# Where the late attention gates are multiplied in, and how many buffers the output units' rows have

## The chip, the cores and the metric

The kernel runs on one core of a Trainium2 chip. The metric is the time of one execution in device microseconds (us); lower is better. A run is one timed execution, and a profiled execution is one more that the hardware profiler recorded.

## The reference

One layer of a hybrid encoder. The input x (2048 rows of 1024) is RMS-normalised and projected once. The columns of the projection feed two groups of heads, and both groups end in a gate:

```python
proj = h @ w_in
(dn_q, dn_k, dn_v, dn_z, dn_beta, dn_decay, sw_q, sw_k, sw_v, sw_z) = split(proj, cuts)
dn = gated_deltanet_bidir(...)                  # 4 heads of 128, forward and backward scans
dn = rms_norm(dn, dn_out_norm_w) * silu(dn_z)
sw = windowed_gqa_with_sinks(...)               # 8 query heads of 64, |i-j| <= 128
sw = sw * silu(sw_z)
x = x + concat([dn, sw]) @ w_out
```

The change concerns sw * silu(sw_z): a product of two arrays of 2048 rows by 512 channels, in fp32.

## The kernel before

All arithmetic is fp32. For the matrix products each operand is split into a high and a low part, so that one product is three matmuls. The sequence is cut into 16 chunks of 128 rows (chunk c), and into four blocks b of 512 rows. Channels of the attention output are four groups f of 128 (two heads each).

**Phase A** (lines 75 to 455) runs over the two halves of the sequence. It makes q, k, v by projections, and for each chunk the windowed attention (`attend`). Beside these, as filler for TensorE, it makes the convolved inputs of the delta rule (`conv_pair`) and the gates of the first half (`gate_pairs`). For chunks 0 to 7 `attend` loads the finished gate (zc, line 407), multiplies on GpSimd (POOL, line 408) and stores the gated output. For chunks 8 to 15 the gates do not exist yet, and the raw output is stored (line 409).

**The late gates** (`late_gates`, lines 230 to 247) make the gates of blocks 2 and 3: sixteen tiles (i, b) in the order of LATE, of which the first eight (i below 4) are attention gates and the others belong to the delta rule (zdn). Each tile takes 24 matmuls into one of three PSUM banks (tag "pj"), a tanh on ACT (line 245), a multiply-add on VectorE (DVE, line 246) and a store (line 247). The tile in SBUF, o, comes from the pool zp, a ring of four buffers with the tag "big". The late gates are traced between the first `pre_front` and the first `solve` of phase B.

**Phase B** goes over the four delta-rule heads h. `pre_front(h)` transposes k, v and q, sums squares on ACT into ssk and ssq (line 690, its throw-away output is jk), and builds the chunks' matrices ma. `solve` inverts 32-row triangles on DVE (lines 749 and 753), `invert` joins them by matmuls (line 781), and `scan(h)` runs forward and backward over the chunks with the state S (lines 821 to 859). `post` normalises the scan's output with squares again (line 873, throw-away output jko) and multiplies by zdn (line 890).

**The output's units** (`sw_units`, lines 564 to 608) are the filler of phase B: 32 units (c, j), each the product of chunk c of the gated attention output with one half j of w_out. A unit loads mx (line 583), for chunks 8 to 15 also the gate zcs (line 586) and multiplies on POOL (line 587), splits into mh and ml (lines 590 and 591), loads a piece of x as xr (named xrs in the trace, line 593), runs 12 matmuls (pcs, lines 596 to 598), adds (line 599) and stores the partial result (line 600). The buffers: mx, mh and ml one each (SWB), and a ring of two (SWW) with the tag "ws" that xr, zcs and the pieces of w_out share. Eight units are traced in each of `pre_front(1)` to `pre_front(3)`, and eight after the last of them.

Last, `out_pair` multiplies the delta rule's output with its part of w_out and adds the partial results.

**What sets the order.** `set_order` plans all instructions of the five queues (TensorE, DVE, ACT, POOL, and SP, which issues all DMAs) at once: it knows the dependences, the rings of buffers and estimates of the durations, goes forward and backward several times, and writes the best order out. Each queue then runs in exactly that order. In the plan an SP transfer is done 2.4 us plus its bytes' time after its issue, a tile of a ring waits for all users of the tile that had its buffer, and no tile begins before the one ahead of it in the ring has begun.

Of the kernel before, what the change touches and what calls it, by code (L numbers as in the profile page):

```python
# [15 lines left out]
P = 128  # L16
# [13 lines left out]
SCRATCH = 1024  # L30
NEG = -1e30
FILLF = ((0, 0, 0, 8), (0, 0, 0, 8), (0, 0, 0, 8))
SWB = (1, 1)
SWW = 2


def tile_hybrid(ctx, tc, t, out, dbg=None):
    nc = tc.nc
    V, A, G, T = nc.vector, nc.scalar, nc.gpsimd, nc.tensor
    dma = nc.sync.dma_start  # L40

    cp = ctx.enter_context(tc.tile_pool(reuse_waits="tile", name="cp", bufs=1))
    gp = ctx.enter_context(tc.tile_pool(reuse_waits="tile", name="gp", bufs=1))
    hp = ctx.enter_context(tc.tile_pool(reuse_waits="tile", name="hp", bufs=2))
    dp = ctx.enter_context(tc.tile_pool(reuse_waits="tile", name="dp", bufs=1, space=DRAM))

    def const(name, shape, src=None, dt=F32):
        a = cp.tile(shape, dt, tag=name, name=name)
        if src is not None:
            dma(a, src)  # L50
        return a

    ident = const("ident", [P, P], t["ident"])
    nw = const("nw", [P, KC], t["nwt"])
    bd = const("bd", [P, NCH, 16])
    mix_sw = [dp.tile([P, 4, P], F32, tag=f"mix_sw{c}", name=f"mix_sw{c}") for c in range(NCH)]
    kq_d = [dp.tile([P, 2, S], F32, tag=f"kq_d{h}", name=f"kq_d{h}") for h in range(4)]
    v_d = [dp.tile([P, S], F32, tag=f"v_d{h}", name=f"v_d{h}") for h in range(4)]
    zdn_d = [dp.tile([P, S], F32, tag=f"zdn{i}", name=f"zdn{i}") for i in range(4)]
    zsw_d = dp.tile([4, P, S], F32, tag="zsw_d", name="zsw_d")  # L60

    mix_dn = dp.tile([4, P, S], F32, tag="mix_dn", name="mix_dn")

    with ExitStack() as cb, ExitStack() as wide:
        with tc.using_default_side("right"):
            xe = cb.enter_context(tc.tile_pool(reuse_waits="tile", name="xe", bufs=1))
            ae = cb.enter_context(tc.tile_pool(reuse_waits="tile", name="ae", bufs=1))
        with ExitStack() as ca:
            consts, late = phase_a(ca, wide, xe, ae, tc, t, ident, nw, bd, gp, mix_sw, kq_d, v_d, zdn_d, zsw_d, dp)
        phase_b(cb, wide, xe, ae, late, tc, t, ident, consts, hp, mix_dn, mix_sw, kq_d, v_d, zdn_d, zsw_d, dp, out)  # L70
    if dbg is not None:
        dbg(tc, locals())


def phase_a(ctx, wide, xe, ae, tc, t, ident, nw, bd, gp, mix_sw, kq_d, v_d, zdn_d, zsw_d, q_pool):
    nc = tc.nc
    V, A, G, T = nc.vector, nc.scalar, nc.gpsimd, nc.tensor
    dma = nc.sync.dma_start
# [151 lines left out]
    def late_gates(zp):  # L230
        held = []
        for i, b in LATE:
            w = next((w for j, w in held if j == i), None)
            if w is None:
                w = [wz.tile([P, KC, P], F32R, tag=k, name=f"{k}{i}_{b}") for k in ("zhi", "zlo")]
                col = (16 + i) // 2 if i < 4 else (8 + i) // 2
                for kk in range(0, KC, 2):
                    st = wz.tile([P, 2, P], F32, tag="zst", name=f"zs{i}_{b}_{kk}", bufs=2)
                    dma(st, t["wt"][col][:, kk : kk + 2, i % 2 * P : (i % 2 + 1) * P])
                    A.activation(w[0][:, kk : kk + 2], st, AF.Copy)  # L240
                    V.tensor_tensor(w[1][:, kk : kk + 2], st, w[0][:, kk : kk + 2].bitcast(F32), ALU.subtract)
                held = (held + [(i, w)])[-2:]
            ps = proj_feat(w, 0, b, f"z{i}_{b}")
            o = zp.tile([P, 512], F32, tag="big", name=f"zo{i}_{b}")
            A.activation(o, ps, AF.Tanh, scale=0.5)
            V.scalar_tensor_tensor(o, o, 1.0, ps, ALU.add, ALU.mult)
            dma((zsw_d[i] if i < 4 else zdn_d[i - 4])[:, b * 512 : (b + 1) * 512], o)

    def conv_pair(i0, half):
        w = load_w(t["wt"][i0 // 2], 2 * P, f"c{i0}_{half}")  # L250
# [107 lines left out]
    def attend(c, q2):  # L358
# [4 lines left out]
        for g in range(2):  # L363
            pr = [sp.tile([P, 3 * P], F32, tag="pr", name=f"pr{c}_{g}_{j}", bufs=6) for j in range(4)]
            st = sp.tile([P, 3, 4], F32, tag="st", name=f"st{c}_{g}")
            nm, den, es = (st[:, i] for i in range(3))
            for j in range(4):
                hh = 4 * g + j
                ps = pss.tile([P, 3 * P], F32, tag="pss", name=f"s{c}_{hh}")
                T.matmul(ps[:, :n], q2[g][:, j], k2[:, g, 0, k0 : k0 + n], start=True, stop=False)  # L370
                T.matmul(ps[:, :n], q2[g][:, j], k2[:, g, 1, k0 : k0 + n], start=False, stop=True)  # L371
                V.tensor_tensor_reduce(  # L372
                    pr[j][:, :n], ps[:, :n], mask[:, lo * P : hi * P], 1.0, sink[:, hh : hh + 1],
                    ALU.add, ALU.min, accum_out=nm[:, j : j + 1],
                )
                A.activation(  # L376
                    pr[j][:, :n], pr[j][:, :n], AF.Exp, bias=nm[:, j : j + 1], scale=-1.0, accum_out=den[:, j : j + 1]
                )
            V.tensor_tensor(es, nm, sink[:, 4 * g : 4 * g + 4], ALU.subtract)
            A.activation(es, es, AF.Exp)  # L380
            V.scalar_tensor_tensor(den, den, 1.0, es, ALU.mult, ALU.add)
            V.tensor_scalar(den, den, 2.0, None, ALU.mult)
            V.reciprocal(den, den)  # L383
            for j in range(4):
                G.tensor_scalar(pr[j][:, :n], pr[j][:, :n], den[:, j : j + 1], 1.0, ALU.mult, ALU.mult)  # L385
            po = pso.tile([P, 512], F32, tag="pso", name=f"po{c}_{g}")
            for kb in range(lo, hi):
                pt = pst.tile([P, 4, P], F32, tag="pst", name=f"pt{c}_{g}_{kb}")
                for j in range(4):
                    T.transpose(pt[:, j], pr[j][:, (kb - lo) * P : (kb - lo + 1) * P], ident)  # L390
                ph = sp.tile([P, 512], F32R, tag="ph", name=f"ph{c}_{g}_{kb}")
                pl = sp.tile([P, 512], F32R, tag="pl", name=f"pl{c}_{g}_{kb}")
                ptf = pt.rearrange("p a b -> p (a b)")
                A.activation(ph, ptf, AF.Copy)  # L394
                V.tensor_tensor(pl, ptf, ph.bitcast(F32), ALU.subtract)  # L395
                vk = v2[:, sl - 1 + kb, g]
                T.matmul(po, vk, ph, start=(kb == lo), stop=False)
                T.matmul(po, vk, pl, start=False, stop=(kb == hi - 1))
            ot = sp.tile([P, 2, P], F32, tag="ot", name=f"ot{c}_{g}")
            pv = po.rearrange("p (a b n) -> p a b n", a=2, b=2)  # L400
            A.activation(ot[0:64], pv[64:128, :, 0], AF.Copy)
            A.activation(ot[64:128], pv[64:128, :, 1], AF.Copy)
            V.tensor_tensor(ot[0:64], pv[0:64, :, 0], ot[0:64], ALU.add)
            V.tensor_tensor(ot[64:128], pv[0:64, :, 1], ot[64:128], ALU.add)
            if c < HC:
                zc = sp.tile([P, 2, P], F32, tag="zc", name=f"zc{c}_{g}", bufs=1)
                dma(zc, zsw_d[2 * g : 2 * g + 2, :, c * P : (c + 1) * P].rearrange("f p s -> p f s"))
                G.tensor_tensor(ot, ot, zc, ALU.mult)
            dma(mix_sw[c][:, 2 * g : 2 * g + 2], ot)

    pend = []
    nfill = ((2, 1, 1, 1, 1, 1, 1, 2), (1, 1, 1, 1, 1, 1, 0, 0))
# [134 lines left out]
def phase_b(ctx, wide, xe, ae, late, tc, t, ident, consts, hp, mix_dn, mix_sw, kq_d, v_d, zdn_d, zsw_d, dp, out):  # L547
# [16 lines left out]
    def sw_units(pool):  # L564
# [12 lines left out]
        def unit(c, j, bank):  # L577
# [3 lines left out]
            ns = slice(j * 512, (j + 1) * 512)  # L581
            mx = pool.tile([P, 4, P], F32, tag="mx", name=f"mxs{c}_{j}", bufs=SWB[0])
            dma(mx, mix_sw[c])
            if c >= HC:
                zc = pool.tile([P, 512], F32, tag="ws", name=f"zcs{c}_{j}").rearrange("p (f s) -> p f s", f=4)
                dma(zc, zsw_d[:, :, c * P : (c + 1) * P].rearrange("f p s -> p f s"))
                G.tensor_tensor(mx, mx, zc, ALU.mult)
            mh = pool.tile([P, 4, P], F32R, tag="mh", name=f"mhs{c}_{j}", bufs=SWB[1])
            ml = pool.tile([P, 4, P], F32R, tag="ml", name=f"mls{c}_{j}", bufs=SWB[1])
            A.activation(mh, mx, AF.Copy)  # L590
# [50 lines left out]
    def pre_front(h):  # L641
# [12 lines left out]
        for n, c4 in enumerate(FRONT):  # L654
# [24 lines left out]
            for j, ss in ((0, ssk), (1, ssq)):  # L679
# [6 lines left out]
                for c in range(4):  # L686
                    cc = 4 * c4 + c
                    src = ks[c4] if j == 0 else tr
                    jk = q1.tile([P, P], F32, tag="jk", name=f"jk{h}_{c4}_{j}_{c}", bufs=3)
                    A.activation(jk, src[:, c], AF.Square, accum_out=ss[:, cc : cc + 1])  # L690
            V.tensor_scalar(ssk[:, s4], ssk[:, s4], EPS, None, ALU.add)  # L691
            G.tensor_tensor(nk[:, s4], ssk[:, s4], pw[:, 0, :4], ALU.pow)  # L692
# [171 lines left out]
    def post(h, H, groups):  # L864
# [4 lines left out]
        so = rp.tile([P, 2, 8], F32, tag="so", name=f"sso{nm}")  # L869
        for k, c4 in enumerate(groups):  # L870
            for c in range(4):
                jk = rp.tile([P, P], F32, tag="jko", name=f"jko{nm}_{k}_{c}", bufs=3)
                A.activation(jk, H["oacc"][c4][:, c], AF.Square, accum_out=so[:, 0, 4 * k + c : 4 * k + c + 1])
        s1 = so[:, 1].rearrange("p (g c) -> p g c", c=4)
        V.tensor_scalar(s1, of(H["ssq"]), EPS, 128.0 * EPS, ALU.add, ALU.mult)
# [541 lines left out]
```

## Time and profile before

| | |
|---|---|
| median of 3 runs | 1264.79 us (1262.38 to 1271.20) |
| profiled execution, its own time | 1270.01 us |
| its span, first to last instruction | 1268.0 us |
| mean granted TensorE clock | 0.989 |
| busy: TensorE / weight loads / DVE / ACT / POOL | 95% / 82% / 75% / 57% / 42% |
| late gates' attention tiles: tanh at | 671.2 to 728.5 us |
| units: first to last matmul | 797.1 to 1169.9 us |

In the profile's rows L587 is line 587 of the kernel, and out<-in names what an instruction writes and reads. PE is TensorE's matmul, PEld its weight load, DVE VectorE, ACT ScalarE, POOL GpSimd, and SPq an instruction of SyncE's queue, here mostly the issue of a DMA. A row of waits reads: who waited, for whom, total us, times, longest us.

### The profile page before, as it was taken

How to read it: one execution, taken by the hardware profiler on the slowest of the kernel's cores; microseconds unless marked ns; L12 is line 12 of the kernel's file. 1: busy time of each engine (PE TensorE's matmuls, PEld its weight loads, DVE VectorE, ACT ScalarE, POOL GpSimd, SP SyncE). 2: the span in 40 equal slices, each digit the busy share in tenths (PEclk: the TensorE clock that was granted, in tenths of full speed). 3: DMA queues.
4: the chain of work that ended last, by engine and by line, in shares of the span. 5: the costliest groups of instructions: out<-in, count | busy, mean ns of one | idle time of the engine just before them, and what ended most of it. 6: DMA issues, size and time to landing. Idle time of an engine off the chain costs nothing.

```text
span 1268.0 us, 22351 instructions
## 1 busy us (share of the span) xinstructions
PE 1210.5 (95%) x7018; PEld 1037.4 (82%) x7018; DVE 953.7 (75%) x2320; ACT 725.8 (57%) x2167; POOL 529.2 (42%) x845
## 2 busy tenths in 40 slices
PE   6999999999999999999999998999889899999898
PEld 5998888788889988887777777888789689888776
DVE  4523689999854379999995587698769779876765
ACT  6432476666534367766665438658557845685421
POOL 2243454763302276556422304613742441670541
PEclk9999999999999999999999999999889999999999
DMA  7553243513544434431016848967955875854785
GB/s 259 172 160 125 75 154 100 173 60 102 166 145 125 144 110 137 137 96 55 34 51 207 238 141 245 264 189 207 268 166 174 236 200 152 242 175 122 238 269 199
DMA packets 232294, 206.39 MB, mean 163 GB/s; under 512 B 49137, under 2 KB 181873, under 8 KB 232177
## 3 DMA queue, kind: packets, MB, share of 16 engines
q1 hardware_dynamic: 232176, 204.97, 53.0%
q8 instruction: 56, 0.92, 0.3%
q14 instruction: 62, 0.50, 0.1%
HBM read 139.84 MB, written 65.08 MB: 162 GB/s over the span
## 4 chain that ended last, share of the span: by engine, by line
PE 67%; DVE 13%; DMA 9%; ACT 4%; issue 3%; POOL 1%; SPq 1%; DVEq 0%; ACTq 0%; POOLq 0%
PE pf_c L199 5%; PE pf_c L201 5%; PE pf_c L200 5%; PE pf_z L199 4%; PE pf_z L200 4%; PE pf_z L201 4%; PE pi L781 3%; PE pq_q L212 2%; PE pq_q L211 2%; PE pt L390 2%; PE pq_q L210 2%; DMA xc<-x_d 2%; PE py L830 2%; PE po L839 2%; PE pcs L596 2%
## 5 line engine op out<-in xcount | busy, mean ns | idle before, releaser
L199 PE MATMUL pf_c<-xhi,wh_c 128*128 128x512 f32 x384 | 155.7, 405 | 0.8 <-DVE acc L269 0.8
L200 PE MATMUL pf_c<-xlo,wh_c 128*128 128x512 f32 x384 | 154.7, 403 | 0.0
L201 PE MATMUL pf_c<-xhi,wl_c 128*128 128x512 f32 x384 | 154.3, 402 | 0.0
L269 DVE SCALAR_TENSOR_TENSOR acc<-pf_c,cw,acc 128x512 f32<-128x512 f32 (+1 forms) x192 | 140.8, 742 | 2.6 <-POOL acc L259 0.7
L385 POOL TENSOR_SCALAR pr<-pr,st 128x384 f32<-128x384 f32 (+1 forms) x128 | 79.4, 639 | 98.0 <-DVE st L383 71.2
L394 ACT ACTIVATE ph<-pt 128x512 fp32r<-128x512 f32 x92 | 53.0, 595 | 60.5 <-PE pt L390 51.5
L376 ACT ACTIVATE pr<-pr,st 128x384 f32<-128x384 f32 (+1 forms) x128 | 76.2, 597 | 17.8 <-DVE st L372 17.4
L199 PEld LDWEIGHTS pf_c<-xhi,wh_c 128*128 128x128 f32 x384 | 72.5, 189 | 13.5 <-DVE acc L269 1.3
L201 PEld LDWEIGHTS pf_c<-xhi,wl_c 128*128 128x128 f32 x384 | 72.3, 188 | 12.9
L200 PEld LDWEIGHTS pf_c<-xlo,wh_c 128*128 128x128 f32 x384 | 72.4, 188 | 11.6
L835 ACT ACTIVATE yk<-py,ck 128x128 f32<-128x128 f32 x120 | 43.9, 366 | 62.0 <-PE py L830 61.2
L372 DVE CUSTOM_DVE_ANT_0 pr<-s,mask,sink 128x384 f32<-128x384 f32 (+1 forms) x128 | 73.4, 593 | 2.5 <-PE s L371 1.0
L211 PE MATMUL pq_q<-wh_q,xlo 128*128 128x256 f32 x256 | 72.1, 282 | 0.0
L212 PE MATMUL pq_q<-wl_q,xhi 128*128 128x256 f32 x256 | 71.9, 281 | 0.0
L210 PE MATMUL pq_q<-wh_q,xhi 128*128 128x256 f32 x256 | 71.4, 280 | 0.0
L390 PE MATMUL pt<-ident,pr 128*128 128x128 f32 x368 | 69.5, 274 | 1.8 <-DVE pl L395 1.1
L395 DVE TENSOR_TENSOR pl<-pt,ph 128x512 fp32r<-128x512 f32 x92 | 61.6, 681 | 6.1 <-ACT ph L394 5.6
L390 PEld LDWEIGHTS pt<-ident,pr 128*128 128x128 f32 x368 | 47.8, 140 | 20.4 <-DVE pl L395 4.4
L596 PE MATMUL pcs<-wohs,mhs 128*128 128x512 f32 x128 | 58.3, 456 | 4.4 <-ACT mhs L590 2.7
L692 POOL TENSOR_TENSOR nk<-ssk,pw 128x4 f32<-128x4 f32 x16 | 16.5, 1029 | 106.8 <-DVE ssk L691 106.6
L597 PE MATMUL pcs<-wohs,mls 128*128 128x512 f32 x128 | 56.1, 438 | 1.7 <-DVE mls L591 1.7
L598 PE MATMUL pcs<-wols,mhs 128*128 128x512 f32 x128 | 55.0, 429 | 0.0
(324 smaller groups left out, 4029.4 us busy)
## 6 DMA issues: line engine op xcount, KB each, us to landing
kqc<-kq_d SPq DMA_DIRECT2D x120, 128.0 KB, 3.1
ws_c<-wt SPq DMA_DIRECT2D x48, 256.0 KB, 3.5
xr<-x SPq DMA_DIRECT2D x16, 512.0 KB, 5.3
k_q<-kq_d SPq DMA_DIRECT2D x16, 512.0 KB, 5.6
mxs<-mix_sw SPq DMA_DIRECT2D x32, 256.0 KB, 3.7
xrs<-x SPq DMA_DIRECT2D x32, 256.0 KB, 3.7
part<-xrs SPq DMA_DIRECT2D x32, 256.0 KB, 2.6
xrd<-part SPq DMA_DIRECT2D x32, 256.0 KB, 4.1
```

Of the source, the lines that this page charges most:

```text
L199: T.matmul(ps, hi[:, k, cs], xhi[b][:, k], start=(k == 0), stop=False)
L200: T.matmul(ps, hi[:, k, cs], xlo[b][:, k], start=False, stop=False)
L201: T.matmul(ps, lo[:, k, cs], xhi[b][:, k], start=False, stop=(k == KC - 1))
L210: T.matmul(ps[:, :n], xh, hi[:, k, :n], start=(k == 0), stop=False)
L211: T.matmul(ps[:, :n], xl, hi[:, k, :n], start=False, stop=False)
L212: T.matmul(ps[:, :n], xh, lo[:, k, :n], start=False, stop=(k == KC - 1))
L269: V.scalar_tensor_tensor(av, ps[:, lo:], cw[:, i, k : k + 1], av, ALU.mult, ALU.add)
L372: V.tensor_tensor_reduce(pr[j][:, :n], ps[:, :n], mask[:, lo * P : hi * P], 1.0, sink[:, hh : hh + 1], ALU.add, ALU.min, accum_out=nm[:, j ...
L376: A.activation(pr[j][:, :n], pr[j][:, :n], AF.Exp, bias=nm[:, j : j + 1], scale=-1.0, accum_out=den[:, j : j + 1])
L385: G.tensor_scalar(pr[j][:, :n], pr[j][:, :n], den[:, j : j + 1], 1.0, ALU.mult, ALU.mult)
L390: T.transpose(pt[:, j], pr[j][:, (kb - lo) * P : (kb - lo + 1) * P], ident)
L596: T.matmul(ps, mh[:, k], wh[:, k], start=(k == 0), stop=False)
```

## The change

- The eight late gates of attention (i below 4 in `late_gates`) now load the raw attention output of their channels and block (mxl, from the same ring zp), multiply it in on POOL and store the gated product. The delta rule's gates stay as they were.
- For that the raw output of chunks 8 to 15 is stored to new DRAM tensors raw_d, laid out by channel group, and the gated product to gat_d, laid out by chunk; `mix_sw[c]` of those chunks is a view of gat_d.
- The units of chunks 8 to 15 load the gated rows and no longer load or multiply a gate.
- mx has two buffers (SWB).
- jk and jko have one buffer each where they had three.

```diff
-SWB = (1, 1)
+SWB = (2, 1)
...
-    mix_sw = [dp.tile([P, 4, P], F32, tag=f"mix_sw{c}", name=f"mix_sw{c}") for c in range(NCH)]
+    mix_sw = [dp.tile([P, 4, P], F32, tag=f"mix_sw{c}", name=f"mix_sw{c}") for c in range(HC)]
...
-    zsw_d = dp.tile([4, P, S], F32, tag="zsw_d", name="zsw_d")
+    zsw_d = dp.tile([4, P, HC * P], F32, tag="zsw_d", name="zsw_d")
+    raw_d = [dp.tile([P, 4, 4, P], F32, tag=f"raw_d{b}", name=f"raw_d{b}") for b in (2, 3)]
+    gat_d = [dp.tile([P, 4, 4, P], F32, tag=f"gat_d{b}", name=f"gat_d{b}") for b in (2, 3)]
+    mix_sw += [gat_d[c // 4][:, c % 4] for c in range(HC)]
...
             A.activation(o, ps, AF.Tanh, scale=0.5)
             V.scalar_tensor_tensor(o, o, 1.0, ps, ALU.add, ALU.mult)
-            dma((zsw_d[i] if i < 4 else zdn_d[i - 4])[:, b * 512 : (b + 1) * 512], o)
+            if i < 4:
+                mx = zp.tile([P, 512], F32, tag="big", name=f"mxl{i}_{b}")
+                dma(mx, raw_d[b - 2][:, i].rearrange("p c s -> p (c s)"))
+                G.tensor_tensor(o, o, mx, ALU.mult)
+                dma(gat_d[b - 2][:, :, i], o.rearrange("p (c s) -> p c s", c=4))
+            else:
+                dma(zdn_d[i - 4][:, b * 512 : (b + 1) * 512], o)
...
-            dma(mix_sw[c][:, 2 * g : 2 * g + 2], ot)
+            dma(mix_sw[c][:, 2 * g : 2 * g + 2] if c < HC else raw_d[c // 4 - 2][:, 2 * g : 2 * g + 2, c % 4], ot)
...
             dma(mx, mix_sw[c])
-            if c >= HC:
-                zc = pool.tile([P, 512], F32, tag="ws", name=f"zcs{c}_{j}").rearrange("p (f s) -> p f s", f=4)
-                dma(zc, zsw_d[:, :, c * P : (c + 1) * P].rearrange("f p s -> p f s"))
-                G.tensor_tensor(mx, mx, zc, ALU.mult)
...
-                    jk = q1.tile([P, P], F32, tag="jk", name=f"jk{h}_{c4}_{j}_{c}", bufs=3)
+                    jk = q1.tile([P, P], F32, tag="jk", name=f"jk{h}_{c4}_{j}_{c}", bufs=1)
...
-                jk = rp.tile([P, P], F32, tag="jko", name=f"jko{nm}_{k}_{c}", bufs=3)
+                jk = rp.tile([P, P], F32, tag="jko", name=f"jko{nm}_{k}_{c}", bufs=1)
```

More of the change, by code (lines that the diff above doesn't have):

```diff
@@ L68, in tile_hybrid @@
         with ExitStack() as ca:
-            consts, late = phase_a(ca, wide, xe, ae, tc, t, ident, nw, bd, gp, mix_sw, kq_d, v_d, zdn_d, zsw_d, dp)
+            consts, late = phase_a(ca, wide, xe, ae, tc, t, ident, nw, bd, gp, mix_sw, kq_d, v_d, zdn_d, zsw_d, raw_d, gat_d, dp)
         phase_b(cb, wide, xe, ae, late, tc, t, ident, consts, hp, mix_dn, mix_sw, kq_d, v_d, zdn_d, zsw_d, dp, out)
@@ L72, in tile_hybrid, with phase_a @@
         dbg(tc, locals())
-def phase_a(ctx, wide, xe, ae, tc, t, ident, nw, bd, gp, mix_sw, kq_d, v_d, zdn_d, zsw_d, q_pool):
+def phase_a(ctx, wide, xe, ae, tc, t, ident, nw, bd, gp, mix_sw, kq_d, v_d, zdn_d, zsw_d, raw_d, gat_d, q_pool):
     nc = tc.nc
```

## The prediction

> **What bounds the kernel now.** I first cut the span into four stages with the busy time of each engine (columns: stretch and its length, then busy time and instruction count of PE, PEld, DVE, ACT, POOL, then granted TensorE clock, DMA share, GB/s).
>
> ```profile
> core 0 of [0], span 1268.0 us
> core 0: us, PE busy (x) PEld busy (x) DVE busy (x) ACT busy (x) POOL busy (x), PEclk, DMA share, GB/s
> 0.00:660.00 660.00, 644.42 (x3609) 550.43 (x3609) 494.88 (x1036) 371.90 (x874) 294.19 (x471) 1.00 0.39 124
> 660.00:790.00 130.00, 124.79 (x617) 101.02 (x615) 90.39 (x253) 73.67 (x280) 34.30 (x49) 1.00 0.67 198
> 790.00:1175.00 385.00, 357.00 (x2432) 319.85 (x2430) 307.80 (x931) 252.94 (x939) 164.17 (x284) 0.97 0.69 200
> 1175.00:1268.00 93.00, 84.25 (x368) 66.07 (x366) 60.66 (x104) 27.26 (x76) 36.50 (x41) 1.00 0.73 236
> ```
>
> TensorE is the bound everywhere, so only its idle time and its lost clock can be won. The change touches two stages: the late gates (660 to 790 us, 5.2 us idle) and the scans with the output's units between them (790 to 1175 us). The second has 385.0 - 357.0 = 28.0 us of idle TensorE and a mean clock of 0.97, which is another 385 x 0.03 = 11.6 us: a ceiling of 39.6 us.
>
> Next, who waited for whom in 790 to 1175 us (total us, times, longest), TensorE first, then the engines that feed the units.
>
> ```profile
> PE gh L702 <- DVE ma L711: 3.8, 3, 2.6
> PE pi L781 <- DVE iv L776: 3.6, 1, 3.6
> PE pcs L596 <- ACT mhs L590: 2.7, 5, 1.0
> PE pcs L597 <- DVE mls L591: 1.7, 3, 0.9
> ...
> POOL mxs L587 <- DMA zcs<-zsw_d: 40.2, 8, 13.8
> ACT mhs L590 <- POOL mxs L587: 6.8, 3, 3.4
> DVE xrs L599 <- DMA xrs<-x: 6.3, 3, 4.2
> ACT mhs L590 <- PE pcs L598: 5.0, 5, 1.7
> ACT mhs L590 <- DMA mxs<-mix_sw: 3.3, 3, 1.3
> ```
>
> The 40.2 us on POOL alone cost nothing. What counts is that the units' matmuls (pcs) waited 2.7 + 1.7 = 4.4 us for their operands, and that DVE stood 4.2 us at once for a unit's residual row (xrs). The timeline around that place shows what such a stand does (start, us, engine, line), and the group of L753 gives that instruction's usual time.
>
> ```profile
> 924.46 0.38 SPq L593 DMA_DIRECT2D xrs<-x  x1
> 931.41 0.69 DVE L599 TENSOR_TENSOR xrs<-xrs,pcs 128x512 f32<-128x512 f32 x1 [4.23 <-DMA xrs<-x]
> 932.31 1.35 POOL L587 TENSOR_TENSOR mxs<-mxs,zcs 128x512 f32<-128x512 f32 x1 [3.99 <-DMA zcs<-zsw_d]
> 932.58 1.21 DVE L753 TENSOR_TENSOR X<-X,tm 128x112 f32<-128x112 f32 x1
> 934.11 0.80 PE L821 MATMUL pk<-S,kqc 128*128 128x128 f32 x2 [3.24 <-DVE S L842]
> ...
> L753 DVE TENSOR_TENSOR X<-X,tm 128x31 f32<-128x31 f32 (+15 forms) x124 | 45.4, 366 | 1.3
> ```
>
> The row is asked for at 924.46 and DVE reaches it too early; behind it in DVE's queue stand the scan's r and S, and TensorE waits 3.24 us for S. After the gap the clock is halved. These rows, of two such places, give the cost:
>
> ```profile
> 930.90:937.70 6.80, 3.60 (x16) 3.50 (x17) 5.12 (x11) 2.18 (x6) 5.13 (x9) 0.66 0.25 79
> 937.70:945.00 7.30, 7.30 (x46) 6.61 (x46) 5.93 (x19) 2.64 (x10) 2.90 (x7) 0.85 0.48 151
> ...
> 1033.20:1036.70 3.50, 2.86 (x12) 2.05 (x13) 2.88 (x9) 2.44 (x9) 3.14 (x8) 0.83 0.80 252
> 1036.70:1044.00 7.30, 7.30 (x46) 6.69 (x45) 5.46 (x19) 3.19 (x11) 1.50 (x5) 0.85 0.35 115
> ```
>
> At the first, 6.80 x 0.34 + 7.30 x 0.15 = 3.4 us of full clock are lost, of which 0.5 us fall into the gap itself (the half-clock stretch is twice 3.4 us, its last 5.8 us are matmuls): 2.9 us. At the second, 3.50 x 0.17 + 7.30 x 0.15 = 1.7 us.
>
> **The change part by part.** *The units (gain).* A unit changes twice. Its input tile mx gets a second buffer, so that its load no longer waits until mls has read the previous one. And for the 16 units of late chunks the gate load zcs and the POOL multiply go away; zcs shared the two "ws" buffers with xrs, so that a late unit's xrs had to wait for the store of the unit before; afterwards two xrs can be under way. What ends as a gain on TensorE:
> - pcs waits: mhs waited 3.3 (load) + 6.8 (multiply) us for things that go, and 5.0 us for TensorE, which stays because mh and ml keep one buffer. Share that goes: 10.1 / 15.1 = 0.67, of 4.4 us: 2.9 us.
> - the wait for S behind xrs: 3.2 us.
> - the two half-clock stretches: 2.9 + 1.7 = 4.6 us.
>
> Sum 10.7 us. From below it is bounded by 0 (in an in-order queue the next wait may stand right behind), from above by the ceiling of 39.6 us. I take 10.7, because these are the rows that name a load the change moves. What is late next are the chains of the inversion (pi <- iv, gh <- ma), which no unit feeds.
>
> *The late gates (cost).* Eight gate tiles now each load 256 KB of raw attention output, multiply on POOL (1.35 us by the row above, 8 x 1.35 = 10.8 us in a stage where POOL is busy 34.3 of 130 us) and store with 512-byte pieces instead of 2 KB ones. The raw output's own stores get smaller pieces too. SP issues eight more loads. These rows show the landing times in 660 to 740 us (of the gate stores, and of a load of the same 256 KB) and when the gates' tanh ran, followed by what POOL waits for in 660 to 790 us:
>
> ```profile
> zsw_d<-zo SPq DMA_DIRECT2D x8, 256.0 KB, 5.3
> k_q<-v_d SPq DMA_DIRECT2D x6, 256.0 KB, 5.9
> ...
> 697.91 0.57 ACT L245 ACTIVATE zo<-pf_z 128x512 f32<-128x512 f32 x1
> 706.92 0.58 ACT L245 ACTIVATE zo<-pf_z 128x512 f32<-128x512 f32 x1
> ...
> 725.60 0.58 ACT L245 ACTIVATE zo<-pf_z 128x512 f32<-128x512 f32 x1
> 727.95 1.10 ACT L245 ACTIVATE zo<-pf_z 128x512 f32<-128x512 f32 x2
> ...
> POOL nk L692 <- DVE ssk L691: 70.0, 7, 24.8
> ```
>
> Both tiles of a gate come from the same ring of four, in the order o, mx, o, mx. The planner lets mx be loaded no earlier than its o is begun, so an o lives 5.9 + 1.35 + 5.3 = 12.6 us, and only two gates fit. At that pace a gate takes 6.3 us; on average there is room (671 to 728 us for seven steps, 8.2 us each), in bursts there is not. Behind a waiting multiply on POOL stand nk and the masks, which have slack (POOL idles 70.0 us before nk); behind a waiting load on SP stand the next weight and k/q loads. Three banks of PSUM let TensorE run three gates ahead, which is the cover. Below: 0. Above, with no cover: the gate after 697.91 and 699.22 is due at 706.92 but gets its tile at 710.5 (3.6 us late), the third of the burst from 725.60 at 738.2 instead of 728.4 (9.8 us): 13.4 us. I take 1.5 us, near the lower end, since the planner knows the ring and can spread the bursts.
>
> Here a rule of the Trainium skill can be weighed. Row: the solve's step L753 took 1.21 us at 932.58, during a POOL multiply, against 0.366 us on average. The Trainium skill, SBUF — State Buffer, section "SBUF: two separate sides", says that a DVE operation with two SBUF inputs and a GpSimd operation that reads SBUF exclude each other for a whole instruction; the trace agrees. By that rule the change takes 16 x 1.35 = 21.6 us of possible blocking away from the scans and puts 10.8 us beside the first solve; my sum counts both as nothing.
>
> *Scratch tiles (cost).* The squares' throw-away outputs jk and jko go from three buffers to one, so each square has to wait for the one before. How much that is shows where ACT reads its own result:
>
> ```profile
> 682.48 0.60 ACT L685 ACTIVATE ks<-tr 128x512 f32<-128x512 f32 x1 [3.81 <-PE tr L682]
> 683.11 0.31 ACT L690 ACTIVATE jk<-ks 128x128 f32<-128x128 f32 x1
> 683.33 0.18 ACT L690 ACTIVATION_READ_ACCUMULATOR jk<-ks 128x1 f32 x1
> 683.42 0.29 ACT L690 ACTIVATE jk<-ks 128x128 f32<-128x128 f32 x1
> ...
> PE trv L719 <- ACT jk L690: 1.6, 2, 0.9
> ...
> 1182.71 0.51 PE L994 MATMUL pcd<-wod,mhd 128*128 128x512 f32 x1 [1.01 <-ACT mhd L988]
> ```
>
> A dependent start comes 0.03 us after the end of its input (683.11 against 683.08), an independent one 0.09 us before the end of its predecessor (683.42 against 683.51): 0.12 us each. There are 4 heads x 4 groups x 8 = 128 of jk and 64 of jko, 192 x 0.12 = 23 us of ACT time at most, 0 if other ACT work fills the holes. A group of eight gets 7 x 0.12 = 0.84 us longer. I charge it where TensorE already waits behind such a group: twice for trv in the gates' stage and once at the end of the last scan, where mhd comes behind eight jko: 3 x 0.84 = 2.5 us.
>
> **Sum.** -10.7 + 1.5 + 2.5 = -6.7 us on the profiled execution's 1270.0 us, that is 1263.3. That execution is 5.2 us above the median of the runs shown (1264.8), so the forecast for the median is 1258.1 us. The first 660 us get no term.
>
> **The rivals.**
> 1. *The freed units also fill the chain gaps.* With mx and xrs there earlier, a unit can stand in the holes of the inversion: pi <- iv 3.6, gh <- ma 3.8, and the rest of the lost clock, 11.6 - 4.6 = 7.0. Half of these 14.4 us gives 7.2 more: 1250.9. For it: of the 28.0 us of idle TensorE I have counted only 6.1 as won. Against it: mh and ml still have one buffer, and the order of the queues is fixed beforehand.
> 2. *The gates' ring sets the pace.* The 13.4 us in place of my 1.5: 1270.0, slower than before. It decides once the bursts stay and gates come closer than 6.3 us. For it: landings of 5 to 6 us in that stage; TensorE is idle for only 5.2 us there, so a delay is not absorbed. Against it: the average pace of 8.2 us, and the three banks.
> 3. *The new order puts a wait where the old one was.* All queues are planned again; if DVE again meets a row or POOL a load that has not landed, with the scan's S behind it, one such place costs 3.2 + 2.9 = 6.1 us. Two of them and no gain: 12.2 + 1.5 + 2.5 = +16.2, 1281.0 us. For it: 39.6 us of such losses exist in an order that was planned with the same rules. Against it: fewer loads per unit leave less to meet.
>
> The change doing nothing that it says can be left out: the loads and multiplies are really gone from the units.
>
> **How the numbers follow.** Forecast 0.42 (own range 1250 to 1265), rival 1 0.25, rival 2 0.15, rival 3 0.18. A measurement of this kernel can tell about 1% from no change, so the borders are 1252.1 and 1277.4 us. Faster: 0.15 of the forecast, 0.24 of rival 1: 0.39. Slower: 0.06 of rival 2 (where the units' gain stays away besides), 0.17 of rival 3: 0.23. Within 1%: 0.38. The range goes from rival 1 with all of its 14.4 us and a little of the small waits (1243, I take 1241) to rival 3 (1281).
>
> **What would show it.** Right: no multiply and no zcs in the units; the waits of pcs under 2 us; no DVE stand over 2 us at xrs; mean clock of the scans' stage at 0.98 or more; POOL busy about 10 us longer in the gates' stage; squares starting 0.41 us apart rather than 0.29. Wrong: TensorE idle more than 10 us in the gates' stage, waiting for zo (rival 2); new waits of several us in front of S, pi or gh with a DMA behind them (rival 3); or a first stage that is not 660 us long within 3 us, since I gave it nothing.

## The result: 0.5% slower, and the profile after

| | before | after |
|---|---|---|
| median, 18 runs each on the same chips | 1263.33 us | 1270.22 us |
| lowest to highest | 1257.88 to 1271.20 | 1264.22 to 1274.11 |
| ratio after / before, 95% interval | | 1.0052 [1.0036, 1.0067] |
| profiled execution, its own time | 1270.01 us | 1272.82 us |
| its span | 1268.0 us | 1271.0 us |

The change costs 6.9 us where 6.7 were forecast as a gain; 1270.2 lies inside the range, on the other side of no change.

The two profiled executions are only 3.0 us apart. That is because the one before was a long one, 6.7 us above its median. The unchanged kernel was therefore profiled once more (run e13 below; its time 1262.59 us, its span 1260.6 us), and this second profile is the fairer partner. First its stages, then those of the changed kernel (columns as in the prediction).

```profile
0.00:660.00 660.00, 643.85 (x3618) 550.29 (x3619) 494.16 (x1041) 372.38 (x876) 294.10 (x471) 1.00 0.38 124
660.00:790.00 130.00, 124.50 (x614) 100.81 (x612) 91.19 (x256) 75.28 (x285) 36.35 (x56) 1.00 0.70 204
790.00:1175.00 385.00, 358.65 (x2452) 319.91 (x2452) 313.71 (x940) 256.89 (x959) 166.76 (x283) 0.98 0.70 205
```

```profile
0.00:660.00 660.00, 642.99 (x3581) 547.69 (x3582) 487.13 (x1020) 367.82 (x865) 294.89 (x467) 0.99 0.39 123
660.00:790.00 130.00, 120.74 (x580) 95.37 (x578) 89.61 (x233) 69.39 (x240) 37.68 (x43) 1.00 0.65 186
790.00:1175.00 385.00, 356.50 (x2445) 318.03 (x2445) 314.54 (x949) 263.25 (x977) 150.38 (x287) 0.98 0.68 197
```

POOL lost its multiplies in the scans (166.8 to 150.4 us). TensorE's idle time did not fall with them: 26.4 us before, 28.5 after. In the gates' stage it rose from 5.5 to 9.3 us. Where each piece of work stands in the span says more than these fixed borders. These are the rows of single instructions' groups (line, engine, operation, count, durations, then first and last start): scores of attention, late gates, units, last stage; the unchanged kernel's second profile first, then the changed kernel.

```profile
L371 PE MATMUL s<-k,q x128: 274/337/426, 138.8 to 664.1; 128*128 128x384 f32 x112, 128*128 128x256 f32 x16
L199 PE MATMUL pf_z<-xhi,zhi x128: 387/389/586, 660.2 to 779.4; 128*128 128x512 f32 x128
L596 PE MATMUL pcs<-wohs,mhs x128: 387/474/988, 793.2 to 1158.4; 128*128 128x512 f32 x128
L994 PE MATMUL pcd<-wod,mh0d x16: 389/390/496, 1169.7 to 1242.5; 128*128 128x512 f32 x16
```

```profile
L380 PE MATMUL s<-k,q x128: 276/337/426, 140.5 to 674.0; 128*128 128x384 f32 x112, 128*128 128x256 f32 x16
L202 PE MATMUL pf_z<-xhi,zhi x128: 386/393/582, 662.4 to 794.4; 128*128 128x512 f32 x128
L601 PE MATMUL pcs<-wohs,mhs x128: 387/474/628, 812.2 to 1175.5; 128*128 128x512 f32 x128
L999 PE MATMUL pcd<-wod,mh0d x16: 389/394/497, 1186.7 to 1253.9; 128*128 128x512 f32 x16
```

The changed kernel starts its last scores 9.9 us later, its last late gate 15.0, its first unit 19.0, its last stage 17.0, and ends 10.4 us later (1271.0 against 1260.6). TensorE's counts in the stages above agree: it has done 37 matmuls fewer by 660 us, 34 fewer in the gates' stage and only 7 fewer in the scans. Attention itself has no edit beyond where its stores go, and it is late already. In the first profile of before the same four places stood at 665.3, 781.2, 797.1 and 1179.0 us: up to the late gates one order comes again within 2 us, behind them within 9.3.

Who waited for whom in 790 to 1175 us of the changed kernel:

```profile
ACT mhs L595 <- PE pcs L603: 10.3, 10, 2.2
...
PE pcs L602 <- DVE mls L596: 4.8, 5, 2.6
...
DVE xrs L604 <- DMA xrs<-x: 3.1, 1, 3.1
```

The waits that the change was to end are gone: mhs waits for no load and no multiply any more, but longer for TensorE (10.3 us, where it was 5.0). The units' matmuls still wait 4.8 us for mls (4.4 us for mhs and mls in the prediction's rows), 2.6 of it in one place:

```profile
841.67 0.69 DVE L604 TENSOR_TENSOR xrs<-xrs,pcs 128x512 f32<-128x512 f32 x1 [3.13 <-DMA xrs<-x]
842.28 0.68 DVE L596 TENSOR_TENSOR mls<-mxs,mhs 128x512 fp32r<-128x512 f32 x1
...
842.88 0.34 DVE L847 SCALAR_TENSOR_TENSOR S<-S,egt,po 128x128 f32<-128x128 f32 x1
...
843.02 0.80 PE L602 MATMUL pcs<-wohs,mls 128*128 128x512 f32 x1 [2.60 <-DVE mls L596]
```

```profile
840.00:843.00 3.00, 0.42 (x4) 0.23 (x3) 1.33 (x3) 1.38 (x5) 1.26 (x1) 0.97 0.87 300
843.00:844.50 1.50, 1.48 (x6) 1.43 (x7) 0.85 (x4) 0.14 (x1) 0.00 (x0) 0.50 0.81 275
844.50:846.00 1.50, 1.50 (x7) 1.40 (x7) 1.17 (x6) 0.44 (x2) 0.00 (x0) 0.50 0.30 113
```

The timeline shows DVE standing at a residual row that has not landed, with mls and the scan's S behind it. The stretches below it show TensorE empty for most of 840 to 843 us and then running at half its clock for the next three. It is the stall that the prediction read at 931 us of the old order, in another place.

### The profile page after: what moved, and what is told of

Read it like the earlier page. It is cut to its first block, busy times and chain, and to the rows that moved or that the text cites. A ratio compares the mean times of both kernels' runs of the same rounds, so it can differ in the third digit from the quotient of the medians.

```text
span 1271.0 us, 22386 instructions
## 1 busy us (share of the span) xinstructions
PE 1211.2 (95%) x7018; PEld 1033.3 (81%) x7018; DVE 958.8 (75%) x2320; ACT 731.9 (58%) x2167; POOL 521.9 (41%) x837
## 4 chain that ended last, share of the span: by engine, by line
PE 61%; DVE 16%; DMA 10%; ACT 6%; issue 4%; POOL 3%; SPq 1%; DVEq 0%; POOLq 0%; ACTq 0%
PE pi L786 4%; PE pf_c L202 4%; PE pf_c L204 4%; PE pf_c L203 4%; PE pf_z L202 3%; PE pf_z L203 3%; PE pf_z L204 3%; DVE acc L278 2%; PE pq_q L215 2%; PE pq_q L214 2%; PE pq_q L213 2%; PE pt L399 2%; PE pcs L602 2%; PE pcs L603 2%; PE pcs L601 2%
## 5 line engine op out<-in xcount | busy, mean ns | idle before, releaser
L202 PE MATMUL pf_z<-xhi,zhi 128*128 128x512 f32 x128 | 51.4, 406 | 6.9 <-ACT zhi L243 4.2
```

Source lines behind the costliest of these rows:

```text
L202: T.matmul(ps, hi[:, k, cs], xhi[b][:, k], start=(k == 0), stop=False)
```

## The experiments

Three theories stood against each other: the **scratch** tiles (each square waits for the one before), the late **gates** (their ring of four tiles), and the **plan** (all queues are ordered anew, and the new order is worse whatever was edited). Ratios are to the kernel before, run on the same chip beside each kernel; the median of the kernel before was between 1261.5 and 1264.6 us there.

| run | what is on the chip | ratio [95%] | median us |
|---|---|---|---|
| e1 | before, one scratch buffer | 1.0178 [1.0147, 1.0209] | 1283.21 |
| e2 | e1 and the second mx buffer | 1.0112 [1.0089, 1.0136] | 1276.50 |
| e3 | before, only the gates moved | 1.0033 [1.0014, 1.0052] | 1266.52 |
| e4, e7, e15 | before, planned with another lag | 1.0056, 1.0051, 1.0092 (each about ±0.002) | 1268.69, 1270.35, 1272.71 |
| e5 | before's order, one scratch buffer | 1.0073 [1.0053, 1.0094] | 1273.44 |
| e6 | three scratch buffers, planned for one | 1.0141 [1.0119, 1.0162] | 1282.30 |
| e8, e16 | after, planned with another lag | 1.0132, 1.0103 (±0.003, ±0.002) | 1280.07, 1274.91 |
| e9 | after's order, two scratch buffers | 1.0052 [1.0027, 1.0077] | 1271.97 |
| e10 | after, two scratch buffers, planned so | 1.0019 [0.9996, 1.0042] | 1267.58 |
| e11 | after, mxl loaded first | 1.0052 [1.0031, 1.0073] | 1272.18 |
| e12 | e10 and e11 | 1.0044 [1.0016, 1.0071] | 1268.64 |
| e13 | before, second profile | | 1262.59 |
| e14 | before's order, second mx buffer | 0.9998 [0.9982, 1.0014] | 1260.64 |
| e17, e18 | e10, planned with another lag | 0.9983 [0.9963, 1.0003], 1.0049 [1.0027, 1.0071] | 1262.42, 1270.79 |

### The parts one by one, each with a new order

e1, from before (jko in the same way):

```diff
-                    jk = q1.tile([P, P], F32, tag="jk", name=f"jk{h}_{c4}_{j}_{c}", bufs=3)
+                    jk = q1.tile([P, P], F32, tag="jk", name=f"jk{h}_{c4}_{j}_{c}", bufs=1)
```

> Theory 1 (the late gates): the kernel before with only jk and jko cut to one buffer is +2.5 us (0 to +4) on the kernel before, by the prediction's own term; the gates' and units' stages keep their ends within 4 us. Theory 2 (the plan): a difference anywhere within 7 us of the kernel before in either direction, with most of it in places that hold no square at all. Theory 3 (the scratch tiles): +7 us, the whole loss, with squares 0.4 us apart and TensorE waits behind them.

e2, on top of it:

```diff
-SWB = (1, 1)
+SWB = (2, 1)
```

> The kernel before with the scratch tiles cut and the second buffer for mx, but the late gates and the units' multiply as before. Theory 1: 4 to 8 us below the first experiment, since this holds part of the units' gain and none of the gates' loss; so -2 to -5 us against the kernel before. Theory 2: anywhere within 7 us either way, unrelated to the first experiment. Theory 3: +7 us or little less.

e3, the changed kernel with `SWB = (1, 1)` and three buffers for jk and jko:

> Only the move of the multiply to the late gates; mx keeps one buffer, jk and jko three. Theory 1: +7 to +12 us against the kernel before, the last late gate's store about 10 us later than 789.6 us, TensorE idle about 9 us in 660 to 790 us. Theory 2: anywhere within 7 us either way. Theory 3: no loss, 0 to -5 us.

e4, the kernel before, where only a constant of the plan differs (e7 and e15 have 2390 and 2380):

```diff
-LAG = {"PE": 205, "DVE": 140, "Activation": 160, "Pool": 120, "SP": 2400}
+LAG = {"PE": 205, "DVE": 140, "Activation": 160, "Pool": 120, "SP": 2410}
```

> No change of the program at all: only the planner's estimate of a transfer goes from 2400 to 2410 ns, so that the order is planned anew. Theory 1 and theory 3: within 2 us of the kernel before. Theory 2: differs by 3 to 8 us in either direction, and the end of the attention moves by several us as it did in the changed kernel (674.3 us instead of 665.6 us).

e4 is the run to remember: the program is unchanged, 10 ns in the plan's idea of a DMA cost 0.56%, as much as the whole change. Each such new order is called a draw below. No difference of half a per cent between two kernels with different orders, then, says anything of their edit. e1's 1.8% is beyond that; e3 is within it, and so is e2's gain on e1 (0.66%).

### Scratch: the wait on the chip, and the wait in the plan

e5 keeps the order of every queue as it was before and changes only the chip's buffers: jk and jko get one each, pad tiles keep the layout, and the plan is told three. e6 is the reverse: three on the chip, one in the plan.

```diff
-            home[f"{tag}_{name}_{p.id}"] = (name, m.bufs)
+            home[f"{tag}_{name}_{p.id}"] = (name, 3 if tag in ("jk", "jko") else m.bufs)
```

> jk and jko have one buffer on the chip, but the planner is told that they have three, and padding keeps the memory's layout: every queue has exactly the order of the kernel before, so that only the real waits between squares are added. If the 19 us of the first experiment are these waits (theory 3), it is again +15 to +20 us. If they are the plan's doing (theory 2), it is +1 to +4 us: 192 squares 0.13 us further apart, mostly off TensorE's path.

> The reverse: three buffers on the chip, but the planner is told one. The order is nearly that of the first experiment, without the real waits. Theory 2: +15 us or more. Theory 3: 0 to +4 us.

> Program of the kernel before, with the planner's estimate of a transfer at 2390 instead of 2400 ns: a second sample of what a mere new order does. Theory 2: -2 to +10 us, most likely slower like the first sample (+4.9 us), because the order of the kernel before is one that was good on the chip. Theories 1 and 3: within 2 us.

> The changed kernel, with the planner's estimate at 2410 instead of 2400 ns. Theory 2: differs from the changed kernel (1.0052 of the kernel before) by more than 3 us either way, so that the loss is not a property of the change. Theory 1: within 2 us of the changed kernel, +5 to +9 us on the kernel before.

In e5 the wait itself costs 0.73%, 9.2 us. ACT's timeline of e5 shows how, beside the squares of before that the prediction quotes (0.31 us apart; the median of all is 0.29):

```profile
683.04 0.31 ACT L690 ACTIVATE jk<-ks 128x128 f32<-128x128 f32 x1
683.26 0.19 ACT L690 ACTIVATION_READ_ACCUMULATOR jk<-ks 128x1 f32 x1
683.48 0.31 ACT L690 ACTIVATE jk<-ks 128x128 f32<-128x128 f32 x1
683.70 0.19 ACT L690 ACTIVATION_READ_ACCUMULATOR jk<-ks 128x1 f32 x1
```

The next square starts 0.03 us after the accumulator of the last was read out (683.48 against 683.45), so the squares are 0.44 us apart. One thing that waits behind a group of eight is TensorE's transpose trv. Its waits from 660 us to the end, first of before, then of e5:

```profile
PE trv L719 <- ACT jk L690: 1.9, 3, 0.9
```

```profile
PE trv L719 <- ACT jk L690: 5.2, 7, 1.4
```

These waits hold 3.3 us of the 9.2. Since the order is the same, the two executions can also be held against each other square by square. The first of the 64 squares before 791 us (eight groups) starts at 683.11 us in before and 683.04 in e5, and the last one at:

```profile
785.56 0.27 ACT L690 ACTIVATE jk<-tr 128x128 f32<-128x128 f32 x1
```

```profile
790.70 0.28 ACT L690 ACTIVATE jk<-tr 128x128 f32<-128x128 f32 x1
```

So e5 falls 5.2 us behind in these eight groups (6.0 us against e13), some 0.7 us a group. Further on the two profiles of before drift apart by more than 9 us, so where the rest of the 9.2 us arises is not shown.

e6 costs 1.41% with no wait on the chip at all, where e1 costs 1.78%; but a part of this is what any new order of before costs (0.51 to 0.92% in e4, e7 and e15). The plan gives the price of a reused buffer as 160 ns of ACT's lag and 90 ns for the second output, 250 ns, where e5 shows 0.44 - 0.31 = 0.13 us from a square's end to the next; it pulls the squares apart and puts other work between them. Counted in the traces, other ACT work stands between two neighbouring squares in 47 of 191 places in before and in 109 in the changed kernel; every order planned for one buffer has 99 to 112 such places, every other order 41 to 55. From the changed kernel:

```profile
693.51 0.26 ACT L695 ACTIVATE jk<-tr 128x128 f32<-128x128 f32 x1
693.67 0.19 ACT L695 ACTIVATION_READ_ACCUMULATOR jk<-tr 128x1 f32 x1
693.76 0.40 ACT L243 ACTIVATE zhi<-zs 128x256 fp32r<-128x256 f32 x1
694.07 0.26 ACT L695 ACTIVATE jk<-tr 128x128 f32<-128x128 f32 x1
```

### Is it the scratch in the changed kernel too?

e9 puts two scratch buffers of half the size into the same bytes of the changed kernel and leaves its order as it is (the plan still counts one); e10 lets the plan know. e11 loads the raw output ahead of the gate's tile; e12 has both.

```diff
-                    jk = q1.tile([P, P], F32, tag="jk", name=f"jk{h}_{c4}_{j}_{c}", bufs=1)
+                    jk = q1.tile([P, P], mybir.dt.bfloat16, tag="jk", name=f"jk{h}_{c4}_{j}_{c}", bufs=2)
```

> The changed kernel, every queue in its own order, with two scratch buffers of half the element size (BF16) for jk and jko in the same bytes, while the plan still counts one. Only ACT's wait for the square before is taken out; the sums of the squares stay fp32. Scratch theory: the 8.9 us that a single buffer cost in the order of before come back, 1261 to 1262 us, ratio to before about 0.998, and squares start 0.29 us apart again. Plan theory: the cost lies in the order, which is the same: 1268 to 1270 us. Gates theory: the same 1268 to 1270 us, with the last gate stored at 801 us as in the changed kernel.

> The same two half-size scratch buffers, with the plan told so and the queues planned again. Scratch theory: the change's own gain is left, about 1260 us. Plan theory: a new draw of the order, 1260 to 1276 us, with no sign fixed beforehand; the last attention scores and the first unit lie some us away from the changed kernel's whichever way. Gates theory: 1266 us or more, since the last gate is stored at 800 us again.

```diff
+            if i < 4:
+                mx = zp.tile([P, 512], F32, tag="big", name=f"mxl{i}_{b}")
+                dma(mx, raw_d[b - 2][:, i].rearrange("p c s -> p (c s)"))
             o = zp.tile([P, 512], F32, tag="big", name=f"zo{i}_{b}")
```

> The changed kernel with mxl allocated and loaded ahead of o in the ring of four, so that the load of the raw output need not wait for the gate's tile to begin. Gates theory: o lives 5.9 us less, the gates' stage gets back up to the 4 us of TensorE's idle time that it gained (9.3 against 5.2 us), 1266 us. Scratch theory: 1270 us, as the squares still wait. Plan theory: anything from 1262 to 1280 us, and the landmarks of attention, ahead of the edit, move too.

> Both edits: two half-size scratch buffers, known to the plan, and mxl loaded ahead of o. If scratch and gates each take their part, 1257 to 1260 us, below the kernel before; if the draw of the order decides, within 1258 to 1276 us with no relation to the runs of the single edits.

The scratch theory as I had written it falls in e9: the squares stand 0.3 us apart again (their starts in the trace: 687.38, 687.69, 687.99) and the time stays where it was, 1.0052. In an order that already keeps the squares apart, the wait on the chip costs nothing that can be measured (e9's interval is ±0.25%), so the loss lies in the order or in the change's other parts. e10 is lower, but within the scatter of the draws. The gates' ring gets no support from e11: same ratio as the changed kernel, and TensorE still waits once for zo. As e11 is a new order too, its ratio cannot exclude a few us; the waits bound what the ring costs TensorE directly, as these rows of 660 to 790 us show, first of the changed kernel, then of e11:

```profile
PE pf_z L202 <- ACT zhi L243: 4.2, 3, 1.6
PE pf_z L202 <- DVE zo L249: 2.4, 1, 2.4
```

```profile
PE pf_z L202 <- ACT zhi L243: 3.6, 3, 2.0
PE pf_z L202 <- DVE zo L252: 2.9, 1, 2.9
```

### Draw against draw

The rest separates the edit from the luck of the order: a second profile of before, the second mx buffer in before's unchanged order (room from half-size scratch, the plan told the old buffers and sizes), and further draws.

> The kernel before, unchanged, for a second profile: the first was taken in an execution of 1270 us, some 6 us above its median. Plan theory: the landmarks of this order (last attention scores 665.6, last gate stored 789.6, first unit 797.1, first matmul of the last stage 1179.0) come again within 2 us, so that their shifts in the changed kernel belong to its order; TensorE's busy time, not its idle time, differs between the two executions. Gates theory: the same. If the landmarks wander by 5 us or more between executions, single profiles cannot place the loss.

> The kernel before, every queue in its own order, with a second mx buffer on the chip that the plan does not know; the room comes from two scratch buffers of half the element size (BF16). The units' gain as predicted (loads in time for mhs): about 3 us for the load's share, 1261 us. Plan theory: nothing measurable, 1263 to 1265 us, because the order was written for one buffer and no SP transfer is issued earlier. Scratch theory: 1264 us as well, since two buffers keep the squares apart.

> The kernel before with only the plan's lag of an SP transfer at 2.38 us instead of 2.40. Plan theory: a third draw of the order of an unchanged program, 1264 to 1275 us, most likely near 1269 us. Gates and scratch theories: 1264 us, nothing of theirs is touched.

> The changed kernel with only the plan's lag of an SP transfer at 2.39 us. Plan theory: another draw, between 1262 and 1281 us, and as far from the changed kernel as the draws of before are from before. Gates and scratch theories: 1270 us within 2 us.

> The changed kernel with two half-size scratch buffers (BF16), known to the plan, and the plan's lag of an SP transfer at 2.41 us. Scratch theory, now in the form that an order planned for one scratch buffer is what costs: like the first draw with two buffers (ratio 1.002) and the draws of the unchanged kernel (1.000 to 1.009), 1262 to 1273 us, and below the draws of the change with one buffer (1.005, 1.010, 1.013). Plan theory, the draw alone: no relation to the number of buffers, 1262 to 1280 us. Gates theory: 1270 us or more.

> The same with the lag at 2.39 us. Scratch theory (an order planned for one buffer costs): 1262 to 1273 us. Draw alone: 1262 to 1280 us. If this or the other draw comes out below 1261 us, it is a version that beats both kernels.

e14 settles the second mx buffer in before's order: 0.9998. The waits of its matmuls did shrink, without moving the end. TensorE's waits in 790 to 1175 us in e13 and in e14:

```profile
PE pcs L596 <- ACT mhs L590: 2.4, 5, 0.7
...
PE pcs L597 <- DVE mls L591: 1.4, 2, 0.9
```

```profile
PE pcs L597 <- DVE mls L591: 2.1, 3, 1.3
...
PE pcs L596 <- ACT mhs L590: 0.8, 2, 0.5
```

For the whole change there are three lags at which before, after and "after with two scratch buffers" were all run:

| lag in the plan | before | after | after, two scratch buffers |
|---|---|---|---|
| 2400 | 1 | 1.0052 | 1.0019 |
| 2410 | 1.0056 | 1.0132 | 0.9983 |
| 2390 | 1.0051 | 1.0103 | 1.0049 |
| mean | 1.0036 | 1.0096 | 1.0017 |

After is above before in each row, by 0.52, 0.76 and 0.52 points: 0.6% of 1264 us is 7.6 us, and this is the change's cost with the draw taken out as far as three draws can. With two scratch buffers it is 0.19% below before, 2.4 us, with rows from -0.73 to +0.19 points: not told apart from nothing. Between the last two columns lie 0.33, 1.49 and 0.54 points, and the load-first pair (e11, e12) gives 0.08: 0.61 on average, 7.7 us. All four kernels with two buffers lie below all four with one. The rest of the record points the same way: the seven orders planned for one buffer (e1, e2, e6, the changed kernel, e8, e11, e16; e1 and e6 are nearly alike) lie 0.52 to 1.78% above before, 1.10% on average, the nine planned for two or three between 0.17% below and 0.92% above, 0.36% on average. So planning for a single scratch buffer costs about as much as the whole loss.

How much the draw adds to a single kernel is as large: before's four draws span 0.92 points, and the order that the comparison starts from is the best of the four. Held against the three redraws alone (0.66% on average), the changed kernel's four orders (e11 with them) cost 0.2 points more, and the four with two buffers 0.4 points less. So of the 6.9 us it stays open how much is the single buffer and how much the good order that before had and any edit would have lost; each alone is large enough.

e17 is the best version found. Its stages:

```profile
660.00:790.00 130.00, 123.77 (x582) 97.20 (x582) 94.86 (x242) 65.64 (x239) 41.18 (x59) 1.00 0.70 200
790.00:1175.00 385.00, 359.23 (x2494) 320.06 (x2492) 310.77 (x945) 261.75 (x973) 142.73 (x267) 0.99 0.68 200
```

TensorE is idle for 6.2 us in the gates' stage, 3.0 less than in the changed kernel, and for 25.8 in the scans. It beats the changed kernel; against before its interval still touches 1. Telling the plan 130 ns in place of 250 for the single buffer was not tried.

## Why the prediction was wrong, by its own steps

- **The new order: put at nothing.** This is the step that failed. The sum has a wait on the chip for the scratch tiles and nothing for planning anew, though the plan knows of the single buffer. e9 shows no cost of that wait in the changed kernel; the draws show 7.7 us for planning with one buffer in place of two, and 6 to 12 us for a mere redraw of before.
- **Scratch tiles, +2.5 us: mis-sized as a wait, too.** The spacing was nearly right (0.41 forecast, 0.44 measured), and so was a group's growth: eight squares took 683.11 to about 685.3 us before and 683.04 to 686.3 in e5, 1.0 us more against 0.84. But I charged three of the 24 groups, those behind which TensorE already waited: two of them, 1.7 us, before 791 us, where e5 falls 5.2 to 6.0 us behind over eight groups. Nearly every group there delayed what follows, and the whole came to 9.2 us.
- **"The planner knows the ring and can spread the bursts": turned round.** I used the plan as cover for the gates and did not ask what it would do with the other edit that it knows. Told of one scratch buffer, its order cost 17.8 us in e6, of which a mere redraw accounts for 6 to 12, where the wait costs 9.2 us when it is just taken; so it does not show that spreading the squares saved anything.
- **The units, -10.7 us: too large.** All that the change does beside the scratch is worth -2.4 us by the table (some -5 us against the redraws of before), where -10.7 + 1.5 was forecast. Term by term: the 2.9 us for pcs came to nothing; in the changed kernel these waits are 4.8 us, and the second buffer alone changes no time in e14, while the multiply's part was not tested in a fixed order. The 3.2 us for S and the clock losses were read from one execution of one order. In e13 the same place looks like this:

```profile
926.51 1.37 DVE L749 TENSOR_TENSOR tm<-L,X 128x112 f32<-128x112 f32 x1
927.91 1.22 DVE L753 TENSOR_TENSOR X<-X,tm 128x112 f32<-128x112 f32 x1
929.06 0.33 DVE L842 SCALAR_TENSOR_TENSOR S<-S,egt,po 128x128 f32<-128x128 f32 x1
```

```profile
926.48 1.27 POOL L587 TENSOR_TENSOR mxs<-mxs,zcs 128x512 f32<-128x512 f32 x1 [1.55 <-ACT oacc L855]
927.70 1.30 POOL L769 TENSOR_TENSOR g<-ma 128x512 f32<-128x512 f32 x1
```

  DVE waited for no row here, and S was late all the same: the two steps of the solve ahead of it (DVE's timeline) ran as long as the two POOL operations beside them (POOL's timeline), and TensorE waited 2.0 us for S. Only one of the two is a unit's multiply; g stays. The Trainium skill, SBUF — State Buffer, section "SBUF: two separate sides", says that a DVE operation with two SBUF inputs and a GpSimd operation that reads SBUF hold each other up for a whole instruction. The trace agrees, and the prediction, which cited this and counted it as nothing, could have found the multiply's half of the wait with it. In the changed kernel a row is late again at 841.67, with 3.13 us: rival 3 in one place.
- **The late gates, +1.5 us.** e3, where only they move, is 0.33% above before and below the three redrawn orders of before; nothing shows a cost beyond a few us. TensorE's idle time in that stage, 9.3 us, stayed under the 10 set for rival 2, and zo accounts for 2.4 of it. That rival 2's 1270.0 us comes so near the measured 1270.2 is luck: it has 13.4 us lost in this stage, where TensorE's idle time grew by 3.8. POOL's busy time there grew by 1.3 to 3.4 us instead of 10, since other POOL work moved out of the stage: eight multiplies came in, and the count fell from 56 (49 in the first profile) to 43.
- **"The first 660 us get no term": wrong.** TensorE's busy time there is within 1.5 us, but attention's last scores came 9.9 us later. e4 moves them as well (669.4 against 664.1) with nothing edited.
- **Rival 3** named the mechanism, the new order, and overpriced it: 16.2 us where about 7 came. A price from redrawn orders of the unchanged kernel would have been 6 to 12 us.
- **Right:** no multiply and no gate load in the units, and a cost of the gates' ring below rival 2's. The clock of 0.98 in the scans' stage was met too, but the second profile of before has 0.98 as well, so it says nothing.

## What to carry to other kernels

Where a planner orders all queues, measure how far an unchanged kernel moves when a constant of the plan moves by half a per cent, before you believe any difference of that size; compare edits in one fixed order, or over several draws, and remember that the order you start from may be a lucky one. A buffer taken from a small operation to pay for a large one is an edit of its own: count all its users, and look at what the plan charges for the reuse. Stalls priced from one execution should be looked up in a second one of the same kernel.

## What the runs showed of the hardware that I had not expected

Two holes of the same size in TensorE's work need not cost the same. The stretches above show the changed kernel's hole at 840 us (0.42 of 3.00 us busy), after which the clock is at half. In the same profile, at 732 us:

```profile
732.00:734.80 2.80, 0.39 (x2) 0.00 (x0) 1.72 (x3) 2.17 (x9) 2.80 (x3) 1.00 0.63 177
734.80:736.30 1.50, 1.48 (x6) 1.24 (x7) 0.56 (x1) 0.31 (x2) 0.50 (x1) 1.00 0.74 137
736.30:737.80 1.50, 1.50 (x8) 1.25 (x7) 0.41 (x1) 0.85 (x4) 1.28 (x1) 1.00 0.91 253
```

Here the clock stays full. What decides is how the hole lies in time. Between its first 40 us and its end, this trace has the clock fall to half at 842.83, 904.27, 1006.67 and 1016.91 us; the steps between these times, 61.44, 102.40 and 10.24 us, are 18, 30 and 3 times 3.413 us, and at each the half clock lasts 3.41 us. So the clock changes at the borders of a fixed grid of windows. Cut at these borders, the two holes (two windows each, first that of 840 us) look like this:

```profile
839.42:842.83 3.41, 1.00 (x8) 0.76 (x7) 1.16 (x2) 1.66 (x7) 1.26 (x1) 1.00 0.79 275
842.83:846.24 3.41, 3.22 (x12) 2.98 (x13) 2.43 (x11) 0.97 (x4) 0.00 (x0) 0.50 0.54 186
730.19:733.60 3.41, 2.14 (x11) 1.32 (x9) 1.87 (x5) 2.06 (x7) 2.31 (x2) 1.00 0.49 139
733.60:737.02 3.42, 2.20 (x10) 1.82 (x11) 1.76 (x3) 1.59 (x8) 2.33 (x3) 1.00 0.76 173
```

The hole at 840 us falls into one window, in which TensorE works for 1.00 us, and half clock follows. The hole at 732 us is cut by a border, and both windows hold over 2.1 us of work. In the twenty traces, after the first 40 us, every window at full clock with less than 1.5 us of work was followed by half clock, and none with more than 2.3 us; between these, both occur. The Trainium skill, TensorE: Matmul & The Clock Gate, section "Part 1: The HAM clock gate (the "warmup" mystery)", lets the clock fall after an idle window of about 3.4 us that runs freely. The trace agrees on the length and on the free running, but the window at 839.42 was not idle, with 1.00 us of work, and there the measurement decides. So the 2.9 us that I charged for the clock behind one stall hold for a hole that leaves one window nearly empty, not for each.

A square with a running sum also holds its output buffer until the sum is read out: 0.13 us beyond its own end in e5.
